# Chunk preparation of an RWKV-7 mixer in three batches, with heads alternating between the row halves of TensorE

## The chip, the cores and the metric

One core of a Trainium2 chip. The metric is the device time of one launch in microseconds (us), median of several runs.

## The reference, cut to what matters

Two layers; in each a token mixer of three groups of heads (stick-breaking attention, latent attention, RWKV-7) over 1024 tokens, and then a gated feed-forward block. The change concerns the RWKV-7 group, 8 heads of 64 channels:

```python
def step(state, inp):
    r_t, w_t, k_t, v_t, kk_t, a_t = inp
    sa = jnp.einsum('bhvk,bhk->bhv', state, -kk_t)
    state = (state * w_t[:, :, None, :] + sa[..., None] * (kk_t * a_t)[:, :, None, :]
             + v_t[..., None] * k_t[:, :, None, :])
    return state, jnp.einsum('bhvk,bhk->bhv', state, r_t)
_, ys = lax.scan(step, init, (tm(rh), tm(wh), tm(kh), tm(vh), tm(kk), tm(ah)))
```

## The kernel before, in words

The recurrence is computed in chunks of 64 tokens. `phase_a` does, for each of four head pairs (`ft`, two heads of 64 channels, one on partitions 0 to 63 and one on 64 to 127): projections of k, r and v (`proj_rw`, lines 202 to 204, matmuls of 512 columns into the tiles `psmm`), `rw_prep`, and then `rw_stage1` twice, once for each half of the sequence (`hf`, 8 chunks). After ft 1 and ft 3, `rw_inv` inverts the triangular blocks of four heads, mostly on VectorE (DVE), in pieces that stand between later projections. `rw_chain` runs the recurrence over chunks afterwards, and reads from DRAM what stage 1 and the inverse stored.

`rw_stage1` first forms decayed keys and queries on DVE, GpSimd (POOL) and ScalarE (ACT): AR (queries) and BK (keys), lines 612 to 638. Then comes the part that the change touches. A call handles two groups `g` of four chunks:

- lines 647, 648: transposes of the queries and a centred transpose of v, into one PSUM tile; ACT copies it to X (line 651) and Vt, a part of Vz (line 652);
- line 655: four transposes of the keys; ACT copies them to RB (line 657);
- line 662, the key-query products: for each head `h` four matmuls with 64 contraction rows, rows 0 to 63 for one head and 64 to 127 for the other, into a PSUM tile of that head; DVE multiplies them by the mask into Aa (line 665) and RB (line 666);
- line 674, 64x64 products of Aa and Vt, eight, which alternate between the two row halves (`e`), into one tile; ACT copies them to X (line 676);
- lines 680, 681: stores of RB and X, and after both groups line 685: stores of Vz, all issued by SyncE (SP).

An fp32 matmul that is no transpose is two passes, and the profile lists the passes: 512 for 256 matmuls. PSUM tiles of this part come from `ps2`, four buffers in all: the tags pa, py, pa, pq in turn.

```python
    def ps2(self):
        self.rot = (self.rot + 1) % 4
        return self.pst(("pa", "py", "pa", "pq")[self.rot])
```

The order on each engine is set when the kernel is built: a scheduler takes instructions of all running steps by priority and expected readiness. The projections of the next head pair fill PE between the steps of stage 1. Engines then run their own list in order.

Of the kernel before, what the change touches and what calls it, by code (L numbers as in the profile page):

```python
# [12 lines left out]
ALU = mybir.AluOpType  # L13
# [4 lines left out]
P = 128  # L18
# [12 lines left out]
C = 64  # L31
NCH = S // C
HC = NCH // 2
# [36 lines left out]
class Body:  # L70
# [31 lines left out]
    def ps1(self):  # L102
        return self.pst("ps")
# [419 lines left out]
    def mla_block(self, i, pr, hp, qk, V, wp):  # L523
# [9 lines left out]
        for u, (a0, a1) in enumerate(pcs):  # L533
# [6 lines left out]
            c = lambda o, u=u: st[:, o + u : o + u + 1]  # L540
            nc.vector.reduce_max(c(0), s, axis=AX.X)
            if u:
# [58 lines left out]
    def rw_stage1(self, ft, hf, rkv, prep, Aa, tp):  # L601
        nc = self.nc
        tk = slice(hf * W2, hf * W2 + W2)
        pr_, pk, pvv = (t[:, tk] for t in rkv)
        L_, av, kk = (t[:, tk] for t in prep)
        ps1 = self.ps2
        Vz = self.Vz[0]
        Vt = Vz.rearrange("p (j x) -> p j x", x=2 * P)[:, :, C : C + P]
        c3 = lambda t: t.rearrange("p (c i) -> p c i", i=C)
        pv4 = lambda t: t.rearrange("p (j e i) -> p j e i", e=2, i=C)  # L610
        G, iG = self.q2(tp), self.q2(tp)
        nc.vector.tensor_scalar(L_, L_, 1.0, None, op0=ALU.add)
        nc.vector.tensor_tensor_scan(L_, self.m01, L_, 0.0, op0=ALU.mult, op1=ALU.add)
        nc.scalar.activation(G, L_, AF.Exp, scale=-0.5 * EC)
        nc.scalar.activation(iG, L_, AF.Exp, scale=0.5 * EC)
        nc.gpsimd.tensor_copy(self.Gc[:, hf * HC : hf * HC + HC, ft], c3(G)[:, :, C - 1])
        AR = self.q4(tp).rearrange("p (a j e i) -> p a j e i", a=2, e=2, i=C)
        BK = self.q4(tp).rearrange("p (j e x i) -> p j e x i", e=2, x=2, i=C)
        kk4, G4, iG4 = pv4(kk), pv4(G), pv4(iG)
        for e in range(2):  # L620
            s_ = 1 - e
            nc.vector.scalar_tensor_tensor(AR[:, 0, :, s_, 1:C], kk4[:, :, e, 1:C], -1.0, G4[:, :, e, 0 : C - 1], op0=ALU.mult, op1=ALU.mult)
            nc.vector.tensor_scalar(AR[:, 0, :, s_, 0:1], kk4[:, :, e, 0:1], -1.0, None, op0=ALU.mult)
            nc.gpsimd.tensor_tensor(AR[:, 1, :, s_, :], pv4(pr_)[:, :, e, :], G4[:, :, e, :], op=ALU.mult)
        nc.sync.dma_start(self.ard[4 * hf : 4 * hf + 4, :, ft].rearrange("j p t -> p j t"), AR[:, 1].rearrange("p j e i -> p j (e i)"))
        nc.vector.scalar_tensor_tensor(kk, av, 1.0, kk, op0=ALU.add, op1=ALU.mult)
        for e in range(2):
            nc.vector.scalar_tensor_tensor(BK[:, :, 1 - e, 1 - e, :], kk4[:, :, e, :], 0.5, iG4[:, :, e, :], op0=ALU.mult, op1=ALU.mult)
        nc.scalar.activation(av, av, AF.Identity, scale=self.om[:, 18 + ft : 19 + ft], bias=self.om[:, 14 + ft : 15 + ft])
        nc.vector.tensor_tensor(av, av, pk, op=ALU.mult)  # L630
        for e in range(2):
            nc.vector.tensor_tensor(BK[:, :, 1 - e, e, :], pv4(av)[:, :, e, :], iG4[:, :, e, :], op=ALU.mult)
        nc.vector.scalar_tensor_tensor(av, pr_, self.pp("rwkv_r_k", ft), av, op0=ALU.mult, op1=ALU.mult)
        ps = ps1()
        self.bsum(ps, av, tp)
        bv = self.q2(tp)
        nc.vector.tensor_tensor(bv, ps, pvv, op=ALU.mult)
        nc.sync.dma_start(self.bvd[4 * hf : 4 * hf + 4, :, ft].rearrange("j p t -> p j t"), bv.rearrange("p (j t) -> p j t", t=P))
        flat = lambda t: t.rearrange("p a i -> p (a i)")
        for g in range(2):  # L640
            js = slice(2 * g, 2 * g + 2)
            RB = self.t(tp, [P, 2, 4, P], "RB", bufs=2)
            X = self.t(tp, [P, 2, 2, P], "X", bufs=2)
            pt = ps1()
            for q in range(2):
                j = 2 * g + q
                nc.tensor.transpose(pt[:, q * P : q * P + P], flat(AR[:, 0, j]), self.ident)
                nc.tensor.matmul(pt[:, (2 + q) * P : (3 + q) * P], pvv[:, j * P : j * P + P], self.cent, start=True, stop=True)
            pa = pt[:, 0:256].rearrange("p (q h k) -> p h q k", q=2, h=2)
            for h in range(2):  # L650
                nc.scalar.copy(X[:, h, :, h * C : h * C + C], pa[:, h])
            nc.scalar.copy(Vt[:, js, :], pt[:, 256:512].rearrange("p (q v) -> p q v", q=2))
            pb = ps1()
            for cc in range(4):
                nc.tensor.transpose(pb[:, cc * P : cc * P + P], flat(BK[:, 2 * g + cc // 2, cc % 2]), self.ident)
            pbv = pb.rearrange("p (c h k) -> p h c k", c=4, h=2)
            nc.scalar.copy(RB[:, :, :, C:P], pbv)
            for h in range(2):
                hr = slice(h * C, h * C + C)
                pA = ps1()  # L660
                for cc in range(4):
                    nc.tensor.matmul(pA[:, cc * P : cc * P + P], flat(BK[hr, 2 * g + cc // 2, cc % 2]), AR[hr, :, 2 * g + cc // 2, cc % 2, :], start=True, stop=True)
                pAv = pA.rearrange("p (c x) -> p c x", x=P)
                mk = self.maskA
                nc.vector.tensor_tensor(Aa[:, h, HC * hf + 4 * g : HC * hf + 4 * g + 4, :], pAv[:, :, 0:C], mk[:, None, 0:C].to_broadcast([P, 4, C]), op=ALU.mult)
                nc.vector.tensor_tensor(RB[:, h, :, 0:C], pAv[:, :, C:P], mk[:, None, C:P].to_broadcast([P, 4, C]), op=ALU.mult)
            pkv = ps1()[:, :256].rearrange("p (h q v) -> p h q v", h=2, q=2)
            for h in range(2):
                for q in range(2):
                    j = 2 * g + q  # L670
                    for e in range(2):
                        kr = slice(64 - 64 * e, 128 - 64 * e)
                        orow = slice(64 * e, 64 * e + 64)
                        nc.tensor.matmul(pkv[orow, h, q, :], Aa[kr, h, HC * hf + 2 * j + e, :], Vt[kr, j, h * C : h * C + C], start=True, stop=True)
            for h in range(2):
                nc.scalar.copy(X[:, h, :, C - h * C : P - h * C], pkv[:, h])
            gj = slice(4 * hf + 2 * g, 4 * hf + 2 * g + 2)
            RBv = RB.rearrange("p h (j e) x -> p h j (e x)", e=2)
            for h in range(2):
                nc.sync.dma_start(self.rbd[gj, :, 2 * ft + h].rearrange("j p x -> p j x"), RBv[:, h])  # L680
                nc.sync.dma_start(self.xxd[gj, :, 2 * ft + h].rearrange("j p x -> p j x"), X[:, h])
        for e in range(2):
            kr = slice(64 - 64 * e, 128 - 64 * e)
            for h in range(2):
                nc.sync.dma_start(self.psd[4 * hf : 4 * hf + 4, kr, 2 * ft + h, e, :].rearrange("j p x -> p j x"), Vz.rearrange("p (j h x) -> p j h x", h=2, x=P)[kr, :, h, :])

    def rw_inv(self, st, tp, Aa):
# [17 lines left out]
        mul = lambda o, x, y: nc.vector.tensor_tensor(o, x, y, op=ALU.mult)  # L705
        red = lambda o, x: nc.vector.tensor_reduce(o, x, axis=AX.X, op=ALU.add)
        for t in range(1, 16):
# [91 lines left out]
    def rw_chain_q(self, st, j, tp):  # L799
        nc = self.nc  # L800
        hs = slice(4 * st, 4 * st + 4)
        fs = slice(2 * st, 2 * st + 2)
        RB = self.t(self.tl, [P, 4, 2, P], "RBl", bufs=2)
        PS = self.t(self.tl, [P, 4, 2, P], "PSl", bufs=2)
        arl = self.t(self.tl, [P, 2, 2, C], "arl", bufs=2)
        bvl = self.t(self.tl, [P, 2, P], "bvl", bufs=Y_LAG + 2)
        nc.sync.dma_start(PS.rearrange("p h e x -> p h (e x)"), self.psd[j, :, hs].rearrange("p h e x -> p h (e x)"))
        nc.sync.dma_start(RB.rearrange("p h e x -> p h (e x)"), self.rbd[j, :, hs])
        nc.sync.dma_start(arl, self.ard[j, :, fs].rearrange("p f (e i) -> p f e i", e=2))
        nc.sync.dma_start(bvl, self.bvd[j, :, fs])  # L810
        QC = self.t(tp, [P, 2, 2, 2, P], "QC", bufs=2)
        PSh = PS.rearrange("p (f h) e x -> p f h e x", h=2)
        RBh = RB.rearrange("p (f h) c x -> p f h c x", h=2)
        for h in range(2):
# [35 lines left out]
    def rw_chain_y1(self, pY, tp):  # L850
# [6 lines left out]
        nc.scalar.activation(yq, ys, AF.Square)  # L857
        nc.vector.tensor_reduce(vs, yq, axis=AX.X, op=ALU.add)
        nc.vector.tensor_scalar(vs, vs, 1.0 / C, GN_EPS, op0=ALU.mult, op1=ALU.add)
# [369 lines left out]
```

## Time and profile before

| | |
|---|---|
| median of 3 runs | 3166.87 us (3161.5 to 3167.62) |
| span of the profiled execution, first to last instruction | 3156.8 us |
| time of that execution beside its span | not given by itself; the median of the runs lies 10.1 us above the span |
| PE busy | 3030.5 us, 96% |
| DVE busy | 1796.4 us, 57% |
| ACT busy | 1060.2 us, 34% |
| mean granted clock of TensorE | 0.984 |

An engine's busy time is the union of its instructions. The profile gives the start of each pass on PE; ends are modelled, so the distance from start to start tells what a pass costs in a row. In rows of the timeline, neighbours of one line and tile are merged (x8), and in brackets stands the idle time of the engine before the first of them, with what ended it.

### The profile page before, as it was taken

To read this page: it belongs to the slowest core of one execution; us is meant where nothing else is said; L and a number is where in the kernel's file an instruction comes from. 1 tells how busy PE (TensorE), PEld (TensorE's weight loads), DVE (VectorE), ACT (ScalarE), POOL (GpSimd) and SP (SyncE) were. 2 spreads that over 40 slices of the span, in tenths; PEclk is the share of its full clock that TensorE was granted. 3 is DMA by queue.
4 is the path that set the end of the run, shared out by engine and by line. 5 is a ranking of instruction groups with operands and counts; after the bars stand their busy time and mean duration, and the time that the engine had idled before them with its cause. 6 is when DMAs were issued, how large, how long until landed. Compare 5 with 4: busy or idle time off the path is not lost. (4 is left out here: it accounts for less than half of the span.)

```text
span 3156.8 us, 42014 instructions
## 1 busy us (share of the span) xinstructions
PE 3030.5 (96%) x16572; PEld 2405.0 (76%) x16572; DVE 1796.4 (57%) x2842; ACT 1060.2 (34%) x1865; POOL 329.9 (10%) x346
## 2 busy tenths in 40 slices
PE   8998999998999999999999989999999999999998
PEld 6676777766888888888877767777668888888887
DVE  4577764777644444444746877567765444344436
ACT  5444343754122111222244443456532211121210
POOL 0112131022000000000001211311310000000000
PEclk9999999999999999999999999999999999999999
DMA  4344666323421111111124356661244111111111
GB/s 129 106 132 117 186 181 185 84 60 122 144 92 47 54 40 47 54 48 53 62 86 124 104 139 192 178 195 46 68 133 172 55 47 40 41 56 51 54 47 54
DMA packets 339284, 301.79 MB, mean 96 GB/s; under 512 B 25224, under 2 KB 304016, under 8 KB 339088
## 3 DMA queue, kind: packets, MB, share of 16 engines
q1 hardware_dynamic: 339088, 299.11, 31.9%
q8 instruction: 131, 2.15, 0.3%
q14 instruction: 65, 0.53, 0.1%
HBM read 208.87 MB, written 90.18 MB: 95 GB/s over the span
## 5 line engine op out<-in xcount | busy, mean ns | idle before, releaser
L202 PE MATMUL psmm<-xTh,whi 128*128 128x512 f32 x2144 | 851.8, 397 | 0.0
L203 PE MATMUL psmm<-xTl,whi 128*128 128x512 f32 x2144 | 851.6, 397 | 0.0
L204 PE MATMUL psmm<-xTh,wlo 128*128 128x512 f32 x2144 | 851.3, 397 | 0.0
L197 ACT CAST whi<-raw 128x1024 fp32r<-128x1024 f32 x152 | 159.9, 1052 | 1108.4 <-PE psmm L203 1085.6
L204 PEld LDWEIGHTS psmm<-xTh,wlo 128*128 128x128 f32 x2144 | 404.9, 189 | 92.8 <-issue 4.4
L203 PEld LDWEIGHTS psmm<-xTl,whi 128*128 128x128 f32 x2144 | 404.9, 189 | 92.7 <-issue 3.9
L202 PEld LDWEIGHTS psmm<-xTh,whi 128*128 128x128 f32 x2144 | 404.5, 189 | 92.8 <-issue 4.4
L198 DVE TENSOR_TENSOR wlo<-raw,whi 128x1024 fp32r<-128x1024 f32 x122 | 148.9, 1220 | 422.1 <-ACT whi L197 422.0
L1031 DVE TENSOR_TENSOR y<-y,psps 128x512 f32<-128x512 f32 x288 | 196.5, 687 | 171.7 <-PE psps L204 171.3
L202 PE MATMUL psps<-wdh,hh 128*128 128x512 f32 x672 | 266.8, 397 | 0.0
L203 PE MATMUL psps<-wdl,hh 128*128 128x512 f32 x672 | 263.1, 391 | 0.0
L204 PE MATMUL psps<-wdh,hl 128*128 128x512 f32 x672 | 260.1, 391 | 0.0
L894 POOL TENSOR_TENSOR lrs<-lrs,mhalf 128x1 f32<-128x1 f32 x32 | 29.1, 910 | 1639.8 <-DVE lrs L893 1639.8
L202 PEld LDWEIGHTS psps<-wdh,hh 128*128 128x128 f32 x672 | 126.1, 188 | 36.6 <-ACT hh L197 5.5
L204 PEld LDWEIGHTS psps<-wdh,hl 128*128 128x128 f32 x672 | 126.1, 188 | 27.1
L203 PEld LDWEIGHTS psps<-wdl,hh 128*128 128x128 f32 x672 | 126.3, 188 | 25.8
L1006 DVE TENSOR_TENSOR cv<-cv,psmm 128x1024 f32<-128x1024 f32 x44 | 53.8, 1222 | 141.9 <-PE psmm L204 136.9
L198 DVE TENSOR_TENSOR wdl<-raw,wdh 128x1024 fp32r<-128x1024 f32 x42 | 51.5, 1225 | 89.9 <-ACT wdh L197 89.9
L198 POOL TENSOR_TENSOR wlo<-raw,whi 128x1024 fp32r<-128x1024 f32 x30 | 75.8, 2528 | 243.5 <-ACT whi L197 243.5
L820 PE MATMUL pspa<-RBl,PSl 128*128 128x128 f32 x512 | 74.6, 295 | 16.5 <-ACT QC L823 10.8
L312 PE MATMUL pspa<-Aa,mv 128*64 128x128 f32 x576 | 84.6, 288 | 4.7 <-ACT Aa L328 4.5
L203 PE MATMUL psmm<-wol,whi 128*128 128x512 f32 x192 | 77.3, 403 | 8.8 <-DVE wol L198 4.6
(443 smaller groups left out, 4757.1 us busy)
## 6 DMA issues: line engine op xcount, KB each, us to landing
raw<-in_ffn_w_up_dram SPq DMA_DIRECT2D x88, 512.0 KB
raw<-in_w_in_dram SPq DMA_DIRECT2D x44, 512.0 KB
raw<-in_ffn_w_down_dram SPq DMA_DIRECT2D x44, 512.0 KB
rbd<-RB SPq DMA_DIRECT2D x64, 256.0 KB
PSl<-psd SPq DMA_DIRECT2D x32, 512.0 KB
RBl<-rbd SPq DMA_DIRECT2D x32, 512.0 KB
psd<-Vz SPq DMA_DIRECT2D x64, 128.0 KB
xxd<-X SPq DMA_DIRECT2D x64, 128.0 KB
```

The costliest lines, as they stand in the source:

```text
L197: self.nc.scalar.copy(hi, src)
L198: (eng or self.nc.vector).tensor_tensor(lo, src, hi.bitcast(F32), op=ALU.subtract)
L202: mm(out, lh, rh, start=start, stop=False)
L203: mm(out, lh, rl, start=False, stop=False)
L204: mm(out, ll, rh, start=False, stop=stop)
L312: self.nc.tensor.matmul(av[hp * 64 : hp * 64 + 64, :], V[:, j, hcol : hcol + 64], wt[:, j, :], start=j == 0, stop=j == nb - 1)
L820: nc.tensor.matmul(pQ[:, f, e, :], PSh[:, f, h, e, :], RBh[:, f, h, e, :], start=True, stop=True)
L894: nc.gpsimd.tensor_tensor(rs, rs, self.mhalf[:, 0:1], op=ALU.pow)
L1006: nc.vector.tensor_tensor(cv, cv, pg, op=ALU.mult)
L1031: nc.vector.tensor_tensor(y[:, i, hs], y[:, i, hs], ps, op=ALU.add)
```

## The change

Both groups are now handled in three batches. RB and X of both groups are taken first. Batch 1: the transposes of both groups. Batch 2: all four key-query tiles of a call are taken at once, and the loop over chunks is outside that over heads, so that heads alternate. Batch 3: the 64x64 products of both groups go into two tiles, one for each `e`; ACT copies each tile's 64 rows by group and head, eight copies a call where there were four of 128 rows. The stores come last.

```diff
+        RBs = [self.t(tp, [P, 2, 4, P], "RB", bufs=2) for _ in range(2)]
+        Xs = [self.t(tp, [P, 2, 2, P], "X", bufs=2) for _ in range(2)]
         for g in range(2):
             js = slice(2 * g, 2 * g + 2)
-            RB = self.t(tp, [P, 2, 4, P], "RB", bufs=2)
-            X = self.t(tp, [P, 2, 2, P], "X", bufs=2)
+            RB, X = RBs[g], Xs[g]
...
+        mk = self.maskA
+        pAs = [[ps1() for h in range(2)] for g in range(2)]
+        for g in range(2):
+            for cc in range(4):
+                for h in range(2):
+                    hr = slice(h * C, h * C + C)
+                    nc.tensor.matmul(pAs[g][h][:, cc * P : cc * P + P], flat(BK[hr, 2 * g + cc // 2, cc % 2]), AR[hr, :, 2 * g + cc // 2, cc % 2, :], start=True, stop=True)
             for h in range(2):
-                hr = slice(h * C, h * C + C)
-                pA = ps1()
-                for cc in range(4):
-                    nc.tensor.matmul(pA[:, cc * P : cc * P + P], flat(BK[hr, 2 * g + cc // 2, cc % 2]), AR[hr, :, 2 * g + cc // 2, cc % 2, :], start=True, stop=True)
...
-            pkv = ps1()[:, :256].rearrange("p (h q v) -> p h q v", h=2, q=2)
+        pks = [ps1() for e in range(2)]
+        for g in range(2):
             for h in range(2):
                 for q in range(2):
-                    j = 2 * g + q
                     for e in range(2):
+                        j = 2 * g + q
                         kr = slice(64 - 64 * e, 128 - 64 * e)
-                        orow = slice(64 * e, 64 * e + 64)
-                        nc.tensor.matmul(pkv[orow, h, q, :], Aa[kr, h, HC * hf + 2 * j + e, :], Vt[kr, j, h * C : h * C + C], start=True, stop=True)
-            for h in range(2):
-                nc.scalar.copy(X[:, h, :, C - h * C : P - h * C], pkv[:, h])
+                        o = ((g * 2 + h) * 2 + q) * C
+                        nc.tensor.matmul(pks[e][64 * e : 64 * e + 64, o : o + C], Aa[kr, h, HC * hf + 2 * j + e, :], Vt[kr, j, h * C : h * C + C], start=True, stop=True)
+        for e in range(2):
+            er = slice(64 * e, 64 * e + 64)
+            pkv = pks[e].rearrange("p (g h q v) -> p g h q v", g=2, h=2, q=2)
+            for g in range(2):
+                for h in range(2):
+                    nc.scalar.copy(Xs[g][er, h, :, C - h * C : P - h * C], pkv[er, g, h])
+        for g in range(2):
```

In the changed file the lines are 648, 649 and 656 (transposes), 652, 653 and 657 (their copies), 664 (key-query), 667 and 668 (masks), 677 (64x64) and 683 (their copies).

What the scheduler makes of it is seen in the order of instructions on each engine. A number behind a tile's name tells buffers apart; in brackets stand the engines whose semaphores an instruction waits for, where it waits. First PE in the first half of ft 1, layer 0, from the last transposes of the keys on (pspa_1654 is head 0's key-query tile, pspy_1661 head 1's). Before:

```order
L655 MATMUL pspq_1648<-ident_60,q_299_1612 128x128 x4
L662 MATMUL pspa_1654<-q_298_1611,q_299_1612 128x128 [waits Pool_49]
L662 MATMUL pspa_1654<-q_298_1611,q_299_1612 128x128 x3
L662 MATMUL pspy_1661<-q_298_1611,q_299_1612 128x128 [waits DVE_49]
L662 MATMUL pspy_1661<-q_298_1611,q_299_1612 128x128 x3
L674 MATMUL pspa_1668<-Vz_182_875,Aa_877 64x64 [waits DVE_49,Activation_49]
L674 MATMUL pspa_1668<-Vz_182_875,Aa_877 64x64 x3
L647 MATMUL pspq_1685<-ident_60,q_298_1611 128x128 [waits Activation_49]
L648 MATMUL pspq_1685<-cent_79,pst_1546 128x128
L674 MATMUL pspa_1668<-Vz_182_875,Aa_877 64x64 [waits DVE_49]
L674 MATMUL pspa_1668<-Vz_182_875,Aa_877 64x64 x3
```

The change:

```order
L656 MATMUL pspy_1672<-ident_60,q_299_1620 128x128 [waits DVE_49]
L656 MATMUL pspy_1672<-ident_60,q_299_1620 128x128 x3
L664 MATMUL pspa_1678<-q_298_1619,q_299_1620 128x128 [waits PE_49,Activation_49,Pool_49]
L664 MATMUL pspq_1679<-q_298_1619,q_299_1620 128x128 [waits Activation_49]
L664 MATMUL pspa_1678<-q_298_1619,q_299_1620 128x128
L664 MATMUL pspq_1679<-q_298_1619,q_299_1620 128x128
L664 MATMUL pspa_1678<-q_298_1619,q_299_1620 128x128
L664 MATMUL pspq_1679<-q_298_1619,q_299_1620 128x128
L664 MATMUL pspa_1678<-q_298_1619,q_299_1620 128x128
L664 MATMUL pspq_1679<-q_298_1619,q_299_1620 128x128
L664 MATMUL pspa_1680<-q_298_1619,q_299_1620 128x128 [waits PE_49,Activation_49]
L664 MATMUL pspy_1681<-q_298_1619,q_299_1620 128x128 [waits Activation_49]
```

Four of one head and four of the other have become pairs, 16 in a row, and no transpose stands between the 64x64 products any more. ft 3 is set out in the same way.

Second, PE in the first half of ft 0, layer 0, from the key-query matmuls on. Before:

```order
L662 MATMUL pspa_1163<-q_220_1120,q_221_1121 128x128 [waits Pool_49]
L662 MATMUL pspa_1163<-q_220_1120,q_221_1121 128x128 x3
L647 MATMUL pspq_1194<-ident_60,q_220_1120 128x128 [waits Activation_49]
L648 MATMUL pspq_1194<-cent_79,pst_1055 128x128
L575 MATMUL pspy_1137<-q_223_1138,bonesr_78 128x512 [waits Activation_49]
L647 MATMUL pspq_1194<-ident_60,q_220_1120 128x128
L674 MATMUL pspa_1177<-Vz_182_875,Aa_877 64x64 [waits DVE_49]
L674 MATMUL pspa_1177<-Vz_182_875,Aa_877 64x64 x3
```

The change:

```order
L664 MATMUL pspa_1179<-q_220_1120,q_221_1121 128x128 [waits PE_49,Activation_49,Pool_49]
L664 MATMUL pspa_1179<-q_220_1120,q_221_1121 128x128 x3
L664 MATMUL pspq_1180<-q_220_1120,q_221_1121 128x128 [waits Activation_49]
L664 MATMUL pspq_1180<-q_220_1120,q_221_1121 128x128
L575 MATMUL pspy_1137<-q_223_1138,bonesr_78 128x512 [waits Activation_49]
L664 MATMUL pspq_1180<-q_220_1120,q_221_1121 128x128 x2
L664 MATMUL pspa_1181<-q_220_1120,q_221_1121 128x128
L576 MATMUL pspy_1137<-q_224_1139,bonesr_78 128x512 [waits DVE_49]
L664 MATMUL pspa_1181<-q_220_1120,q_221_1121 128x128 x3
L677 MATMUL pspa_1207<-Vz_182_875,Aa_877 64x64 [waits DVE_49,PE_49]
```

Here the scheduler still puts a whole head ahead of the other, with sums of another step (lines 575, 576) between; the source alternates, the list does not.

Third, ACT in the first half of ft 0, layer 0, of the change, from the second copy of v to the end of that half (Vz holds v, RB_1147 and RB_1148 are the two groups' tiles):

```order
L653 COPY Vz_182_875<-pspa_1165 128x2x128
L197 CAST whi_1549<-raw_1548 128x1024
L657 COPY RB_1147<-pspq_1159 128x8x64
L197 CAST q_223_1138<-ta_943 128x512
L302 ACTIVATE pst_1383<-psmm_1413,om_69_293 128x512
L614 ACTIVATE q_240_1245<-tw_942 128x512
L615 ACTIVATE q_241_1246<-tw_942 128x512
L657 COPY RB_1148<-pspy_1173 128x8x64
L683 COPY X_1149<-pspa_1207 64x2x64 x2
L683 COPY X_1150<-pspa_1207 64x2x64 x2
L683 COPY X_1149<-pspq_1208 64x2x64 x2
L683 COPY X_1150<-pspq_1208 64x2x64 x2
```

A weight cast (line 197) stands ahead of the copy to RB that frees a PSUM buffer for the key-query matmuls, and the eight copies of 64 rows stand together at the end.

## Rows read from the trace of the kernel before

**Rows 1.** The page, busy time by engine.

```profile
PE 3030.5 (96%) x16572; PEld 2405.0 (76%) x16572; DVE 1796.4 (57%) x2842; ACT 1060.2 (34%) x1865; POOL 329.9 (10%) x346
```

**Rows 2.** Table by stretch (us: length, busy by engine, granted clock, DMA share, GB/s).

```profile
143.00:173.00 30.00, 28.40 (x220) 22.26 (x221) 23.50 (x46) 16.98 (x40) 4.51 (x4) 1.00 0.60 173
189.00:215.00 26.00, 24.66 (x206) 19.80 (x205) 18.03 (x35) 11.22 (x31) 4.17 (x4) 1.00 0.67 197
215.00:253.00 38.00, 31.89 (x131) 24.79 (x130) 36.36 (x60) 15.21 (x19) 6.83 (x5) 0.91 0.18 46
336.00:362.00 26.00, 24.60 (x205) 19.77 (x204) 18.57 (x34) 10.96 (x31) 7.65 (x18) 1.00 0.68 202
```

**Rows 3.** Timeline of PE, first half of ft 1 (start us, length us, instruction).

```profile
191.02 0.82 PE L662 MATMUL pspa<-q,q 64*128 64x128 f32 x5
191.57 0.37 PE L662 MATMUL pspy<-q,q 64*128 64x128 f32 x1
191.68 0.27 PE L662 MATMUL pspa<-q,q 64*128 64x128 f32 x1
191.79 0.27 PE L662 MATMUL pspy<-q,q 64*128 64x128 f32 x1
...
192.01 0.72 PE L662 MATMUL pspy<-q,q 64*128 64x128 f32 x5
193.96 0.45 PE L674 MATMUL pspa<-Vz,Aa 64*64 64x64 f32 x8 [1.23 <-DVE Aa L665]
194.34 0.33 PE L647 MATMUL pspq<-ident,q 128*128 128x128 f32 x1
```

**Rows 4.** Timeline of PE, second half of ft 1, one head between projections.

```profile
202.86 0.40 PE L204 MATMUL psmm<-xTh,wlo 128*128 128x512 f32 x1
203.09 0.40 PE L202 MATMUL psmm<-xTh,whi 128*128 128x512 f32 x1
203.42 1.16 PE L662 MATMUL pspq<-q,q 64*128 64x128 f32 x8
204.51 0.50 PE L203 MATMUL psmm<-xTl,whi 128*128 128x512 f32 x1
204.84 0.40 PE L204 MATMUL psmm<-xTh,wlo 128*128 128x512 f32 x1
205.08 0.39 PE L575 MATMUL pspa<-q,bonesr 128*128 128x512 f32 x1
```

**Rows 5.** Timeline of PE, first half of ft 0, 64x64 products.

```profile
156.18 0.68 PE L674 MATMUL pspq<-Vz,Aa 64*64 64x64 f32 x16
156.79 0.50 PE L202 MATMUL psmm<-xTh,whi 128*128 128x512 f32 x1
```

**Rows 6.** Timeline of DVE, masks of the first half of ft 1.

```profile
193.40 0.41 DVE L665 TENSOR_TENSOR Aa<-pspa,maskA 128x256 f32<-128x256 f32 x1
193.73 0.41 DVE L666 TENSOR_TENSOR RB<-pspa,maskA 128x256 f32<-128x256 f32 x1
...
197.31 0.42 DVE L665 TENSOR_TENSOR Aa<-pspy,maskA 128x256 f32<-128x256 f32 x1 [2.51 <-PE pspy L662]
...
198.31 0.42 DVE L666 TENSOR_TENSOR RB<-pspa,maskA 128x256 f32<-128x256 f32 x1
```

**Rows 7.** Timeline of ACT, copies of ft 1.

```profile
190.85 0.42 ACT L651 COPY X<-pspa 128x128 f32<-128x128 f32 x2
...
191.42 0.62 ACT L657 COPY RB<-pspq 128x512 f32<-128x512 f32 x1
...
195.31 0.43 ACT L676 COPY X<-pspa 128x128 f32<-128x128 f32 x2 [2.23 <-PE pspa L674]
...
205.94 0.59 ACT L657 COPY RB<-pspa 128x512 f32<-128x512 f32 x1 [0.94 <-PE pspa L655]
```

**Rows 8.** Groups of PE: line, tiles, shape, count, busy us, mean ns, idle before.

```profile
L674 PE MATMUL pspa<-Vz,Aa 64*64 64x64 f32 x256 | 14.3, 229 | 8.3 <-DVE Aa L665 7.9
```

**Rows 9.** Timeline of SP, a store of RB in the first half of ft 1.

```profile
200.16 0.44 SPq L680 DMA_DIRECT2D rbd<-RB  x1
```

More of the change, by code (lines that the diff above doesn't have):

```diff
@@ L655, in rw_stage1 @@
                 nc.tensor.transpose(pb[:, cc * P : cc * P + P], flat(BK[:, 2 * g + cc // 2, cc % 2]), self.ident)
-            pbv = pb.rearrange("p (c h k) -> p h c k", c=4, h=2)
-            nc.scalar.copy(RB[:, :, :, C:P], pbv)
-            for h in range(2):
-                hr = slice(h * C, h * C + C)
-                pA = ps1()
-                for cc in range(4):
-                    nc.tensor.matmul(pA[:, cc * P : cc * P + P], flat(BK[hr, 2 * g + cc // 2, cc % 2]), AR[hr, :, 2 * g + cc // 2, cc % 2, :], start=True, stop=True)
-                pAv = pA.rearrange("p (c x) -> p c x", x=P)
-                mk = self.maskA
+            nc.scalar.copy(RB[:, :, :, C:P], pb.rearrange("p (c h k) -> p h c k", c=4, h=2))
@@ new lines, in rw_stage1 @@
+        mk = self.maskA
[5 more added lines that the diff above has]
+                    nc.tensor.matmul(pAs[g][h][:, cc * P : cc * P + P], flat(BK[hr, 2 * g + cc // 2, cc % 2]), AR[hr, :, 2 * g + cc // 2, cc % 2, :], start=True, stop=True)
+            for h in range(2):
+                pAv = pAs[g][h].rearrange("p (c x) -> p c x", x=P)
@@ L665, in rw_stage1 @@
                 nc.vector.tensor_tensor(Aa[:, h, HC * hf + 4 * g : HC * hf + 4 * g + 4, :], pAv[:, :, 0:C], mk[:, None, 0:C].to_broadcast([P, 4, C]), op=ALU.mult)
-                nc.vector.tensor_tensor(RB[:, h, :, 0:C], pAv[:, :, C:P], mk[:, None, C:P].to_broadcast([P, 4, C]), op=ALU.mult)
-            pkv = ps1()[:, :256].rearrange("p (h q v) -> p h q v", h=2, q=2)
+                nc.vector.tensor_tensor(RBs[g][:, h, :, 0:C], pAv[:, :, C:P], mk[:, None, C:P].to_broadcast([P, 4, C]), op=ALU.mult)
@@ L677, in rw_stage1 @@
+        for g in range(2):
             gj = slice(4 * hf + 2 * g, 4 * hf + 2 * g + 2)
-            RBv = RB.rearrange("p h (j e) x -> p h j (e x)", e=2)
+            RBv = RBs[g].rearrange("p h (j e) x -> p h j (e x)", e=2)
             for h in range(2):
                 nc.sync.dma_start(self.rbd[gj, :, 2 * ft + h].rearrange("j p x -> p j x"), RBv[:, h])
-                nc.sync.dma_start(self.xxd[gj, :, 2 * ft + h].rearrange("j p x -> p j x"), X[:, h])
+                nc.sync.dma_start(self.xxd[gj, :, 2 * ft + h].rearrange("j p x -> p j x"), Xs[g][:, h])
```

## The prediction

> **What bounds the kernel now.** I read the page's busy shares first: TensorE (PE) is busy for 96% of the span [rows 1], so what shortens PE's queue, or a wait in front of it, shortens the kernel, and nothing else does by itself. The changed function runs 16 times (two layers, four head pairs ft, two halves hf of the sequence), in pairs of calls that I call bursts. The table by stretch shows three bursts and the stretch behind the second [rows 2]: inside a burst PE is busy for 24.7 of 26 us, so a burst is PE's own work; in 215 to 253 us DVE is busy for 36.4 of 38 us and PE for 31.9, at a granted clock of 0.91 of 2.4 GHz, which means short spells at 1.2 GHz. There DVE's block inverse leads, and it can start only when the burst's last mask is done. A burst that ends sooner on both engines is therefore worth its full length; one that ends sooner on PE alone is not.
>
> PE's instructions one by one come next, for the first half of ft 1. A key-query matmul is two passes, 64 rows of the array each; the passes of one head start 0.11 us apart, and the second head's first pass (191.57, tile pspy) starts while four passes of the first head are still to be run [rows 3]. The two row halves run side by side, and a half that is free starts up to four passes early. So four matmuls of one head behind four of the other take 1.55 us (191.02 to 192.46, and the last 0.11), not 1.9. One head alone takes 1.09 us from its first pass to the next instruction, of which 0.89 is eight passes. The rest is change of shape: matmuls of 512 columns stand 0.23 apart, but 0.33 ahead of the 64-row ones and again behind the first of the next shape [rows 4]. Each change of array shape costs two times 0.10 us, 0.10 ahead of it and 0.10 behind its first pass.
>
> The 64x64 products are paired already: 16 passes end 0.61 us after the first starts, 8 passes 0.38 (193.96 to 194.34) [rows 5, 3], so eight more cost 0.23, which is 0.058 a pair.
>
> **The change part by part.** I count on PE's listing of both kernels, since the listing and not the source says who stands beside whom.
>
> 1. *Key-query matmuls.* Of 256, 20 stand directly behind one of the other head before, 116 now, but unevenly. With 0.112 us a pass and 0.10 for the first of each half: the first half of ft 1 or ft 3 goes from two stretches of 4+4, 2 x 1.54 = 3.08 us, to one fully alternating stretch of 16 matmuls, 16 passes deep, 1.89. The second half goes from 0.99 + 0.99 + 1.54 = 3.53 to 0.77 (a stretch of three) + 1.89 (thirteen, eight of them on one head) = 2.66. Each such burst saves 2.06, four of them 8.2. In ft 0 and ft 2 the scheduler still sets out whole heads: 7.18 to 6.83 and 7.16 to 7.27 a burst, together 0.5 less over both layers. Sum: -8.7.
> 2. *Changes of shape* at the lines of the key-query and 64x64 products: 190 before, 156 now, 34 x 0.20 = 6.8; of that 0.8 lies in item 1 (48 stretches became 40). Sum: -6.0.
> 3. *64x64 products*: in 16 places the two row halves no longer stand next to each other in the listing, 16 x 0.116 = +1.9. The new second PSUM tile itself gives nothing, as they are paired already. Both halves write one tile before the change, and still start as pairs. The Trainium skill (TensorEngine Tiling (Array Packing), Gotcha 1: PSUM Pressure) says that different row tiles cannot access one PSUM bank at the same time; by that rule the split would bring these products a pairing that they lack. The trace does not agree: 64 columns at 0.112 / 128 us each are 0.056, so two passes in 0.058 are side by side.
> 4. *Masks on DVE*: the same 128 instructions. In the first half of ft 1 the first mask starts at 193.40, held by DVE's own work before it, and the last at 198.31, after 2.51 us of waiting for the second group's matmuls [rows 6]. With both groups' matmuls ahead, eight masks 0.33 apart start last at 195.7: 2.6 us sooner. So DVE follows PE in ft 1 and ft 3 and gives the saving on to the block inverse.
> 5. *Copies on ACT*: 64 more, of 64 rows x 128 elements, which the trace does not show. From below they cost nothing where ACT is idle; from above 0.27 each as the 128-row ones alone, 17 us in all; those 128-row ones come 0.16 apart in a row. I take nothing on the path: ACT sat idle for 2.23 us before such a copy [rows 7]. With that cover gone, the tiles of the 64x64 products come free some 0.3 to 0.6 us later in each call, at most 16 x 0.6 = 10 us.
> 6. *Waits in front of key-query matmuls.* All four PSUM buffers now go to the second batch, so it waits for ACT's copies of both groups. One group's copies take 1.2 us (190.85 to 192.04) [rows 7], two 2.4, done at 193.2; the first eight alternating matmuls, begun when one group is copied, end at 193.0. I take 0.1 to 0.5 us a call, against the waits of 1.2 us that PE has now in front of the 64x64 products, 7.9 us in six places [rows 3, 8], which go where masks come earlier. I set the two equal: 0, with -8 and +16 (1 us a call) as ends.
> 7. *Transfers*: the same number and size. The last store of RB of the first half is issued at 200.16, and ACT fills the next RB of the second half from 205.9 on [rows 9, 7]; masks that end 2.6 us sooner lengthen that distance. I cost it at nothing.
>
> Sum: -8.7 - 6.0 + 1.9 = -12.8 us. The profiled execution would go from a span of 3156.8 to 3144.0; the median of the runs stands 10.1 above that span, so I predict 3154.0 us. The first item leans on rows: by the Trainium skill (TensorE: Matmul & The Clock Gate, Part 3) matmuls start strictly in program order, which the pass at 191.57 contradicts; by that rule the kernel before would have fewer passes side by side, and item 1 would be -9.8 (44 matmuls of 0.223 us).
>
> **The rivals.**
> - *The saved PE time comes back as waits.* Masks (eight at 0.33, 2.7 us a call) take longer than alternating matmuls (1.9), so PE reaches the 64x64 products early and waits. For it: that wait exists today in front of them [rows 8]. Against it: items of filler stand between them, and DVE itself waited 2.5 us for PE [rows 6]. Then items 1 and 3 fall away, and of item 2 some two thirds stay: about 3163. The Trainium skill says that row tiling speeds up TensorE and not the emptying of PSUM (TensorEngine Tiling (Array Packing), PSUM Bottleneck); that is this rival. Chance 0.22.
> - *Slower: four buffers are too few.* The second batch cannot begin until ACT has emptied the first, and in the listing ACT puts a weight cast ahead of one of those copies in ft 0, and PE's queue stands behind it. It decides from 0.8 us a call on (12.8 / 16). At 1.5 us a call it is +24 - 12.8 = +11: 3178. For it: PE is in order, and ACT now has 64 more copies there. Against it: ACT is busy for 11 of 26 us in ft 1 [rows 2]. Chance 0.12.
> - *More than the sum.* PE's present waits go without new ones (-5 to -8), and shorter idle keeps the clock at 2.4 GHz behind the bursts, where 9% of 38 us were lost in this stretch alone [rows 2]: 3141. Should the 64x64 products nevertheless gain from a tile for each half, by half of their 512 passes at 0.029 us, it is another 7 us: 0.02 of this case. Chance 0.14.
>
> **How the numbers follow.** The forecast, 3154 give or take 6, gets 0.52. About 0.2% (6 us, also the spread of the three runs) is what a measurement of this kernel can tell from no change: faster takes the forecast and the larger gain, 0.66; same is the first rival, 0.22; slower the second, 0.12. The range goes from 3138, the larger gain with some room, to 3168, which takes in the first rival and leaves out most of the second.
>
> **What would show it.** Right: in ft 1 and ft 3 key-query passes of two tiles start in pairs, 16 matmuls in about 1.9 us; the last mask of a burst comes 2 to 4 us sooner after its first transpose; PE's busy time falls by about 10 us or more; bursts of ft 0 and ft 2 stay as they are. Wrong: waits of PE for ACT in front of the key-query line of over 0.8 us a call, or waits in front of the 64x64 products that grow by what the matmuls saved.

## The result, and the profile after

| | before | after |
|---|---|---|
| median on one chip, us | 3161.5 (7 runs, 3154.0 to 3167.7) | 3178.75 (7 runs, 3170.2 to 3183.4) |
| ratio, 95% interval | | 1.0051 [1.0038, 1.0065] |
| span of the profiled execution, us | 3156.8 | 3177.0 |
| mean granted clock of TensorE | 0.984 | 0.976 |

The change makes the kernel 0.5% slower. The forecast was 3154 us, and 3178.75 lies outside the range of 3138 to 3168.

Busy time by engine on the page after, which answers to [rows 1]:

```profile
PE 3050.0 (96%) x16572; PEld 2420.3 (76%) x16572; DVE 1788.1 (56%) x2842; ACT 1069.4 (34%) x1929; POOL 329.3 (10%) x346
```

PE has the same 16572 instructions and is busy for 19.5 us longer, almost the whole 20.2 us of the span. So over the whole kernel the passes have become longer; PE's idle time hardly changes (127.0 us, where it was 126.3).

The first half of ft 1 went nearly as forecast. PE's timeline after, first half of ft 1, answers to [rows 3]:

```profile
199.42 0.60 PE L656 MATMUL pspy<-ident,q 128*128 128x128 f32 x4
199.95 0.37 PE L664 MATMUL pspa<-q,q 64*128 64x128 f32 x1
199.96 0.37 PE L664 MATMUL pspq<-q,q 64*128 64x128 f32 x1
200.16 0.27 PE L664 MATMUL pspa<-q,q 64*128 64x128 f32 x1
200.17 0.27 PE L664 MATMUL pspq<-q,q 64*128 64x128 f32 x1
...
201.78 0.38 PE L664 MATMUL pspy<-q,q 64*128 64x128 f32 x2
202.11 0.30 PE L677 MATMUL pspa<-Vz,Aa 64*64 64x64 f32 x2
```

Passes of the two heads start 0.01 us apart, and all 16 key-query matmuls take 2.16 us up to the next instruction (forecast: about 1.9). DVE's masks answer to [rows 6]; they now stand in a row, without the 2.51 us wait:

```profile
201.23 0.41 DVE L667 TENSOR_TENSOR Aa<-pspa,maskA 128x256 f32<-128x256 f32 x1
...
203.21 0.41 DVE L667 TENSOR_TENSOR Aa<-pspy,maskA 128x256 f32<-128x256 f32 x1
203.54 0.41 DVE L668 TENSOR_TENSOR RB<-pspy,maskA 128x256 f32<-128x256 f32 x1
```

From this half's first transpose to the start of its last mask it is 5.9 us (197.66 to 203.54), where it was 8.5 (189.83 to 198.31).

The first half of ft 0 did not. The table by stretch (us: length, busy by engine, granted clock, DMA share, GB/s) over the first 22 us of ft 0, before and then after:

```profile
143.00:151.00 8.00, 6.45 (x44) 5.17 (x45) 7.81 (x12) 4.15 (x8) 2.70 (x1) 1.00 0.10 18
151.00:165.00 14.00, 14.00 (x104) 10.98 (x103) 10.76 (x25) 8.27 (x20) 1.80 (x3) 1.00 0.76 220
```

```profile
143.00:151.00 8.00, 6.34 (x43) 5.10 (x43) 6.73 (x15) 5.71 (x13) 2.97 (x2) 1.00 0.30 66
151.00:165.00 14.00, 14.00 (x65) 10.43 (x65) 6.79 (x18) 3.34 (x11) 1.59 (x2) 0.51 0.48 148
```

PE is busy for all 14 us in both, but it gets through 65 instructions where it was 104, at a granted clock of 0.51, that is 1.2 GHz of 2.4 for nearly the whole stretch (151.3 to 165.0 us). PE's timeline after shows what stood ahead of the fall at 151.3 us:

```profile
146.90 0.66 PE L656 MATMUL pspq<-ident,q 128*128 128x128 f32 x4
147.49 0.93 PE L664 MATMUL pspa<-q,q 64*128 64x128 f32 x6
...
148.87 0.50 PE L575 MATMUL pspy<-q,bonesr 128*128 128x512 f32 x1
...
150.77 0.50 PE L576 MATMUL pspy<-q,bonesr 128*128 128x512 f32 x1 [0.76 <-DVE q L198]
151.21 1.13 PE L664 MATMUL pspa<-q,q 64*128 64x128 f32 x4
...
152.70 1.11 PE L677 MATMUL pspa<-Vz,Aa 64*64 64x64 f32 x8
...
157.89 2.07 PE L664 MATMUL pspy<-q,q 64*128 64x128 f32 x8
```

From 146.90 to 151.2 stand four transposes, 18 passes of 64 rows, two matmuls of 512 columns and one wait of 0.76 us. The queries' transposes of both groups are done by then; before the change those of the second group, 64x64 products and projections stood among these passes. Behind the fall eight key-query passes take 2.0 us (157.89 to the next instruction at 159.90), where one head took 1.09 [rows 4], and DVE waits for them, 5.72 us in all, with the other work that stands ahead of them:

```profile
160.00 0.42 DVE L667 TENSOR_TENSOR Aa<-pspy,maskA 128x256 f32<-128x256 f32 x1 [5.72 <-PE pspy L664]
```

Where the 20.2 us came from, by the starts of the first transposes, the chain's first matmul (L820 before, L828 after) and the first matmul of the latent attention, in the two profiled executions; in brackets the time at 1.2 GHz within the stretch:

| stretch | layer 0 before | after | layer 1 before | after |
|---|---|---|---|---|
| ft 0 to ft 1 | 46.7 (0) | 53.8 (13.7) | 47.9 (3.4) | 53.7 (13.7) |
| ft 1 to ft 2 | 63.2 (6.8) | 60.8 (6.8) | 63.4 (10.2) | 59.3 (6.8) |
| ft 2 to ft 3 | 83.1 (10.2) | 84.5 (13.7) | 83.7 (10.2) | 88.6 (23.9) |
| ft 3 to the chain | 36.8 (0) | 33.9 (0) | 37.0 (0) | 34.5 (0) |
| the chain stretch | 173.1 (10.2) | 179.0 (17.1) | 165.9 (6.8) | 172.6 (17.1) |

The stretches that begin with ft 1 and ft 3 gain 11.9 us. Those of ft 0 and ft 2 lose 19.2, and the chain stretch, whose code is the same, loses 12.6. That is 19.9 of the 20.2. Each column is one execution, and where the clock falls differs between executions; the runs below repeat these stretches in other kernels.

### The profile page after: what moved, and what is told of

Same layout as the page of the kernel before. It is cut to its first block, busy times and chain, and to the rows that moved or that the text cites. A ratio compares the mean times of both kernels' runs of the same rounds, so it can differ in the third digit from the quotient of the medians.

```text
span 3177.0 us, 42078 instructions
## 1 busy us (share of the span) xinstructions
PE 3050.0 (96%) x16572; PEld 2420.3 (76%) x16572; DVE 1788.1 (56%) x2842; ACT 1069.4 (34%) x1929; POOL 329.3 (10%) x346
## 5 line engine op out<-in xcount | busy, mean ns | idle before, releaser
L203 PEld LDWEIGHTS psps<-wdl,hh 128*128 128x128 f32 x672 | 126.3, 188 | 25.7
L1014 DVE TENSOR_TENSOR cv<-cv,psmm 128x1024 f32<-128x1024 f32 x44 | 53.7, 1221 | 143.9 <-PE psmm L204 138.9
L828 PE MATMUL pspa<-RBl,PSl 128*128 128x128 f32 x512 | 73.5, 293 | 18.8 <-ACT QC L831 12.8
L312 PE MATMUL pspa<-Aa,mv 128*64 128x128 f32 x576 | 84.5, 288 | 4.7 <-ACT Aa L328 4.5
L828 PEld LDWEIGHTS pspa<-RBl,PSl 128*128 128x128 f32 x512 | 66.4, 201 | 27.2 <-ACT QC L831 15.5
```

The source lines that it names most:

```text
L203: mm(out, lh, rl, start=False, stop=False)
L312: self.nc.tensor.matmul(av[hp * 64 : hp * 64 + 64, :], V[:, j, hcol : hcol + 64], wt[:, j, :], start=j == 0, stop=j == nb - 1)
L828: nc.tensor.matmul(pQ[:, f, e, :], PSh[:, f, h, e, :], RBh[:, f, h, e, :], start=True, stop=True)
L1014: nc.vector.tensor_tensor(cv, cv, pg, op=ALU.mult)
```

## The experiments

Theory A: the change gains in ft 1 and ft 3, and loses in ft 0 and ft 2 because the clock falls there. Rivals: B, four PSUM buffers are too few (the prediction's second rival), so that each call waits; C, what is worse is the order that the scheduler gives to later steps, the chain above all. The ratios below are to the kernel before on the same chip; chips differ by a few us, so runs are compared by their ratios.

**The change in ft 1 and ft 3 only**, and then **in ft 0 and ft 2 only** (`ft % 2 == 0` in the condition). Lines without a mark are the old code, moved to the right.

```diff
+        if ft % 2:
+            RBs = [self.t(tp, [P, 2, 4, P], "RB", bufs=2) for _ in range(2)]
...
+        else:
             for g in range(2):
                 js = slice(2 * g, 2 * g + 2)
                 RB = self.t(tp, [P, 2, 4, P], "RB", bufs=2)
...
```

> The new code for ft 1 and 3 only, the old code for ft 0 and 2. Theory A (the change gains about 3 us in each burst of ft 1 and ft 3 and loses in ft 0 and ft 2, where the clock falls to 1.2 GHz): faster than before, 4 bursts x 2.8 = 11 us less, about 3150 where before has 3161, ratio 0.996 to 0.998; no long half-clock stretch near 151 and 1725 us. Theory B (four buffers are too few, each call waits): slower than before, some half of the 17 us, about 3170. Theory C (the order of later steps, above all of the chain, is what is worse): no faster than before, with the chain stretch of the second inverse still some 4 us longer in each layer.

> The new code for ft 0 and 2 only, the old code for ft 1 and 3. Theory A: slower than the whole change, 17 + 11 = about 28 us above before, 3185 to 3190, with half-clock stretches near 151 and 1725 us. Theory B: about 3170, half of the loss. Theory C: depends on the chain; the burst of ft 0 itself is no longer than before by more than 2 us.

Measured: 3154.6 us, ratio 0.9982 [0.997, 0.9993], and 3178.7, 1.0057 [1.0036, 1.0078]. The loss goes with the new code in ft 0 and ft 2, as A has it, though the second run lost 18 us and not the 28 that A expected. B falls: it lets every call lose. But the first run gained 6 us, about half of the 11 expected. In its profile the stretches from ft 0 to the chain are 7.3 and 7.9 us shorter than before, and the chain stretch is 4.8 and 4.5 longer, which is C's mark. In the run with ft 0 and ft 2 the chain stretch is about that of before (175.2 and 165.8).

**Alternation alone**, group by group as before:

```diff
-            for h in range(2):
-                hr = slice(h * C, h * C + C)
-                pA = ps1()
-                for cc in range(4):
+            pAs = [ps1() for h in range(2)]
+            for cc in range(4):
+                for h in range(2):
+                    hr = slice(h * C, h * C + C)
...
```

> Alternation alone: in each group the two key-query tiles are taken together and heads alternate; groups follow each other as before, one tile for the 64x64 products. Theory A: the gain of the pairs (4 x about 0.45 us a burst in ft 1 and ft 3, a little in ft 0 and ft 2) without the loss of ft 0, so 3150 to 3158 where before has 3161. Theory B: no loss either, since a group's second batch needs two buffers of four; 3155 to 3161. Theory C: anything between 3150 and 3180, with the chain as the place.

**Batches alone**, the changed kernel with the loops swapped:

```diff
-            for cc in range(4):
-                for h in range(2):
+            for h in range(2):
+                for cc in range(4):
```

> Three batches as in the change, but head 0's four matmuls of a group before head 1's. Theory A: the loss of ft 0 and ft 2 stays, the gain of ft 1 and ft 3 falls by some 1 to 2 us a burst: 3180 to 3188. Theory B: the same, since the buffers are the same. If alternation itself did the harm (its 64-row matmuls leave the array half as long busy), it would be faster than the change: 3160 to 3170.

Measured: 3155.9, 0.9979 [0.9965, 0.9992], and 3155.4, 0.9988 [0.9975, 1.0002]. The second was missed by both theories: two loops swapped take 0.6%, some 20 us, off the changed kernel. The expectation's last case, that alternation itself does the harm, had the direction, but not the size (3160 to 3170). The steps ahead of the chain give little of it. From ft 0 to the chain it takes 232.0 and 232.1 us, the changed kernel 233.0 and 236.2, and its clock falls in ft 0 as well. Its chain stretch is 169.0 and 162.2, against 179.0 and 172.6. So the order of later steps can carry the sign, and the next runs asked what sets it.

**The change in ft 1 only, and in ft 3 only** (the conditions `ft == 1` and `ft == 3`).

> The new code for ft 1 only. In the run with ft 1 and ft 3 the bursts and what lies between them gave 6 to 8 us a layer, and the chain stretch behind ft 3 took 5 back. Theory C1 (the new order in ft 3's burst is what changes the order of the second inverse against the chain): here the chain stretch is as before (173 and 166 us from the chain's first matmul to the latent attention's), the bursts give 3 to 4 us a layer, together 6 to 8 us faster, ratio about 0.998. Theory C2 (any change upstream does it): the chain stretch is again 5 us longer, no gain.

> The new code for ft 3 only. Theory C1: the burst gives 3 us a layer, the chain stretch takes 5: 3160 to 3165, no faster than before, with a half-clock stretch in the chain near 445 and 2015 us. Theory C2 or none: 3 us a layer faster, 3154.

Measured: 3153.6, 0.9988 [0.9977, 0.9999], and 3157.9, 1.001 [0.9999, 1.0021]. With ft 1 alone the chain stretch stays (173.9 and 166.1); with ft 3 alone it grows (176.3 and 169.5) and eats what the burst gained. C1 holds for the chain; the first run's gain, 4 us, is again about half of the 6 to 8 expected (its profiled execution, 3160.6 us, was its slowest, with 10.2 us at 1.2 GHz between ft 3 and the chain of layer 0 and 13.7 in ft 0 of layer 1). The listings say the same: from the first to the last query product of the chain, the sequence of lines and operations on PE and on DVE takes one of four forms in all kernels of this study, and only the code of ft 3 decides which.

| order of the chain, by ft 3's code | runs | chain stretch, layer 0 | layer 1 | of it at 1.2 GHz |
|---|---|---|---|---|
| the code before | before and two | 173.1 to 175.2 | 165.8 to 166.1 | 10.2; 6.8 |
| alternation alone | one | 171.9 | 166.7 | 6.8; 6.8 |
| the change | after and four | 176.3 to 179.0 | 168.7 to 172.6 | 13.7 to 17.1; 10.2 to 17.1 |
| batches, whole heads | four (three of them below) | 169.0 to 172.4 | 162.2 to 164.7 | 3.4 to 10.2; 3.4 to 6.8 |

The change's range lies above that of the code before in both layers, that of whole heads below it. In layer 0 the gaps are small (1.1 and 0.7 us), and alternation alone is one run. This allows a forecast for kernels that had not run:

**The whole change, but whole heads in ft 3.**

```diff
+        if ft == 3:
...
+                for h in range(2):
+                    hr = slice(h * C, h * C + C)
+                    for cc in range(4):
...
+        else:
...
                 for cc in range(4):
                     for h in range(2):
                         hr = slice(h * C, h * C + C)
...
```

> The whole change with one loop swapped back in ft 3 alone: three batches there too, but head 0's four matmuls of a group before head 1's. By the listings the order on TensorE and VectorE from the first to the last matmul of the chain's query products is one of four, and only the code of ft 3 decides which: as before, as in the change, as with alternation alone, as with whole heads in batches. Theory C1 (this order is what the chain stretch costs): the stretch from the chain's first matmul to the latent attention's goes from 179.0 and 172.6 us in the whole change to about 169 and 162, as in the run with whole heads; in all 18 to 20 us faster than the whole change, about 3158 to 3161, no slower than before. Rival (the chain's loss comes from what the burst in ft 0 and ft 2 did to clock and transfers upstream): 3175 to 3180.

Measured: 3155.1, 0.9993 [0.9978, 1.0008]. Two loops swapped in one of four head pairs, and the kernel is no longer slower than before, 0.6% (18 us) under the changed kernel's ratio of 1.0051. The 18 to 20 us were expected with a chain stretch of about 169 and 162; it came to 172.4 and 164.7, which is 14.5 us less than in the changed kernel, so some of the 18 lies elsewhere. In the profiles another 7.3 us stand ahead of the chain of layer 1, most of them where ft 2, whose code is that of the changed kernel, had 10.2 us at 1.2 GHz instead of 23.9. The table by stretch shows the chain stretch of layer 0 in the changed kernel, and then in this one:

```profile
376.90:555.90 179.00, 163.57 (x1423) 131.48 (x1424) 102.70 (x226) 64.08 (x123) 40.71 (x37) 0.95 0.59 179
```

```profile
375.80:548.20 172.40, 158.35 (x1425) 126.27 (x1425) 100.66 (x221) 64.22 (x124) 42.01 (x37) 0.99 0.59 185
```

Both start within 1.1 us of each other. PE is busy 5.2 us longer in the first, at 0.95 instead of 0.99, and idle 1.4 us longer. In the changed kernel the clock falls three times within this stretch, at 383.4, 451.7 and 550.7 us, for 6.8, 6.8 and 3.4 us; the kernel before has falls near its start and end too (380.2 and 540.6), and the one in the middle is new. PE's timeline there; L760 is the inverse, L855 the chain:

```profile
446.48 0.40 PE L202 MATMUL psmm<-xTh,whi 128*128 128x512 f32 x1
448.24 0.76 PE L760 MATMUL pspi<-Aa,pd 32*32 32x32 f32 x36 [1.36 <-DVE Aa L751]
448.93 0.33 PE L855 MATMUL pspy<-S,QC 128*64 128x64 f32 x2
449.19 0.24 PE L760 MATMUL pspi<-Aa,pd 32*32 32x32 f32 x2
...
451.79 0.31 PE L760 MATMUL pspi<-Aa,pd 32*32 32x32 f32 x2
452.03 0.47 PE L855 MATMUL pspy<-S,QC 128*64 128x64 f32 x2
```

and the same place with whole heads in ft 3 (L812 the inverse, L880 and L899 the chain):

```profile
443.03 1.13 PE L880 MATMUL pspa<-RBl,PSl 128*128 128x128 f32 x8 [0.29 <-DVE mo L941]
443.92 0.47 PE L203 MATMUL psmm<-xTl,whi 128*128 128x512 f32 x1
444.93 1.07 PE L812 MATMUL pspi<-Aa,pd 32*32 32x32 f32 x54 [0.54 <-DVE Aa L803]
446.25 0.45 PE L899 MATMUL pspy<-S,QC 128*64 128x64 f32 x8 [0.26 <-DVE S L902]
```

In the first, 1.4 us of waiting and then 4.7 us of small matmuls, 36 of the inverse and then turns of two with the chain. In the second, the waits are shorter, 54 of them stand in a row, and query products of 128x128 are right ahead. Why the scheduler comes to the one or the other from a different last burst was not followed up.

**Is the clock a cause or only goes along?** In ft 0 and ft 2 one matmul of 512 columns was put into each key-query tile ahead of its own, which overwrite it:

```diff
+            if ft % 2 == 0:
+                for h in range(2):
+                    nc.tensor.matmul(pAs[g][h], self.identr, self.lora[0][:, 0:512], start=True, stop=True)
```

> The whole change, and in ft 0 and ft 2 one matmul of 512 columns into each key-query tile ahead of its key-query matmuls, which overwrite it: 32 more matmuls of 0.23 us, 7.4 us of pure extra work. Theory A (the clock is what the change loses in ft 0 and ft 2): these bring PE's array to work there; the half-clock stretches at 151 us (13.7 us), 1725 us (13.7) and 1868 us (13.7) shrink or go, worth up to 20 us together, so the kernel is no slower than the whole change and probably 5 to 12 us faster, 3167 to 3175. Theory B (waits for buffers, or the order alone): 7 to 10 us slower than the whole change, 3186 to 3189, the low stretches being a consequence of the waits. In both the chain stretch stays some 5 us a layer longer than before.

Measured: 3178.8, 1.0072 [1.006, 1.0084]; by ratio that is 0.2%, some 7 us, above the changed kernel, with intervals that just overlap. In total time A, which expected 5 to 12 us less, was wrong, and B's 7 to 10 us more came nearer; the profile has to tell why. The first 22 us of ft 0:

```profile
143.00:151.00 8.00, 7.67 (x49) 5.97 (x50) 5.90 (x14) 5.12 (x12) 0.20 (x1) 1.00 0.26 56
151.00:165.00 14.00, 12.19 (x91) 9.28 (x92) 11.43 (x22) 6.61 (x19) 4.15 (x3) 1.00 0.67 194
```

The fall is gone from ft 0, in both layers, and from first transpose to first transpose the first half takes 15.2 us, where the changed kernel took 20.1 and 19.4 and the kernel before 14.6 and 16.1. So in this half of ft 0 the clock is the loss, and the fall goes when PE is given these matmuls. As a repair it is worthless. The stretch from ft 0 to ft 1 takes 51.3 us at full clock, with PE busy for 49.5 against 45.2 before: of these 4.3 us the eight added matmuls are 1.8 at 0.23 each, and the rest was not taken apart. In ft 2 the time at 1.2 GHz came to 17.1 us in both layers (13.7 and 23.9 in the changed kernel), so what makes the loss there was not shown by this run.

What the fall costs is seen without any edit. Up to ft 1 the runs with the change in ft 1 only and in ft 1 and ft 3 have the same order on PE, the kernel's before. In layer 1 the clock fell in the first of them, and not in the other:

```profile
1707.40:1759.70 52.30, 50.79 (x292) 40.61 (x293) 36.87 (x67) 26.99 (x52) 8.70 (x8) 0.87 0.45 121
```

```profile
1706.90:1753.20 46.30, 44.75 (x292) 35.66 (x293) 36.85 (x67) 27.03 (x52) 8.71 (x8) 1.00 0.52 137
```

13.7 us at 1.2 GHz cost 6.0 us, 0.44 us for each. By the Trainium skill (TensorE: Matmul & The Clock Gate, Part 1) time at half clock costs half of itself; that gives an estimate of 6.9, and the trace agrees roughly. So with the old order the clock can fall too, but seldom does: of twelve stretches of ft 0 with the old code two had over 4 us at 1.2 GHz. With the change, whole heads in batches, or one tile for the products it was nine of ten. With alternation alone it was none of two, so the fall goes with the batches and not with the alternation.

**One tile for the 64x64 products** of a group, and four copies on ACT as before, the rest as changed.

```diff
-        pks = [ps1() for e in range(2)]
+        for g in range(2):
+            pkv = ps1()[:, :256].rearrange("p (h q v) -> p h q v", h=2, q=2)
```

> The whole change, but the 64x64 products of a group in one tile with four copies a call on ACT, as before the change. Theory A: the 64 extra copies and the split matter little; within 5 us of the whole change, 3174 to 3182. If the two tiles and the eight copies were what costs (each tile waits for both groups' masks), it is faster by 8 us or more: below 3171.

Measured: 3170.0, 1.0042 [1.0026, 1.0059], an interval that overlaps the changed kernel's [1.0038, 1.0065]. Its 3170 us lie just under the 3171 that was to speak for a cost of the copies, but by ratio it is 0.09%, some 3 us, under the changed kernel, where 8 were asked. So the 64 copies and the second tile are at most a side issue; up to some 0.1% for them stays open. In layer 1 the clock did not fall in ft 0, and that stretch took 46.8 us, as before the change: in this order the batches cost nothing where the clock stays up.

**Two kernels put together from this**: old code in ft 0 and ft 2, whole heads in batches in ft 3, and in ft 1 either the change or whole heads too. The second is the run with batches alone, with one condition more:

```diff
+        if ft % 2:
             RBs = [self.t(tp, [P, 2, 4, P], "RB", bufs=2) for _ in range(2)]
...
                 for h in range(2):
                     hr = slice(h * C, h * C + C)
                     for cc in range(4):
...
+        else:
+            for g in range(2):
...
```

> Old code in ft 0 and ft 2, the change in ft 1, three batches with whole heads in ft 3. Theory A and C1 together: the bursts and what lies between give 6 to 8 us a layer as in the run with ft 1 and ft 3, the chain stretch gives 4 a layer as with whole heads: 20 to 24 us faster than before, 3134 to 3142, ratio 0.9925 to 0.9945. Rival (gains do not add, the chain's order is worth something only behind the other bursts): 3150 to 3157.

> Old code in ft 0 and ft 2, three batches with whole heads in ft 1 and ft 3. Batching gave 2.9 us in a burst of ft 1 with whole heads too, though its 16 key-query matmuls take 2.8 us where alternating ones take 2.2. Theory: within 4 us of the run with the change in ft 1 and whole heads in ft 3: 3134 to 3145. If alternation is what gains in ft 1: some 3 us a layer slower than that run.

Measured: 3141.3, 0.9949 [0.9936, 0.9963], and 3139.5, 0.9942 [0.9927, 0.9956]. Gains of bursts and of the chain's order add up, if not fully: the first run is 16 us faster than before, where 20 to 24 were expected, and its ratio is just above the 0.9925 to 0.9945 forecast. The second run, within 4 us of the first as expected, beats both kernels, by 0.6% and 1.1%, and it has no alternating heads at all. Its busy times:

```profile
PE 3017.1 (96%) x16572; PEld 2396.5 (76%) x16572; DVE 1792.4 (57%) x2842; ACT 1063.3 (34%) x1897; POOL 332.4 (11%) x346
```

PE's 13.4 us less against [rows 1] are close to the 12.8 that the change was forecast to save, but by another way: part of them is the chain, which the forecast left out.

## Why the prediction was wrong

- *Item 1, key-query matmuls: right in size, in the wrong part.* In the first half of ft 1 they went from 1.71 + 1.71 to 2.21 us (first start to last modelled end), 1.21 less; forecast was 1.19. By the forecast's own measure, with the last pass at 0.11 us, it is 3.10 to 2.05, 1.05 less. With whole heads in batches it is 2.82: half of the saving comes from the batch, half from alternation. Alternation's half is worth nothing in time here: from the first half's first transpose to the second's it is 8.0 us with it, 7.6 without, 10.5 before. In that one point the first rival, saved PE time that comes back, was right.
- *Item 4, masks: right.* The last mask of this half comes 2.6 us sooner after its first transpose, as forecast, and the stretches from ft 1 and ft 3 gain 2.4 to 4.1 us each, 11.9 in all. In the largest, 4.1, 3.4 us less at 1.2 GHz have a part. Item 2, changes of shape, was not measured by itself.
- *Items 3 and 5, 64x64 products and copies: not contradicted.* The +1.9 of item 3 was not measured by itself. Two tiles give no pairing that one lacks: eight passes start within 0.23 us in either (204.25 to 204.48 after; 0.45 less the last pass's own 0.22 in [rows 3]), and the run with one tile and four copies was at most some 3 us faster.
- *Item 6, waits: set to 0, and too cautious.* The new waits that it allowed in front of the key-query matmuls did not come: the list of PE's waits after has no row for L664. Waits in front of the 64x64 products went from 7.9 us in six places [rows 8] to 2.4 (all rows of L677), which is the gain that the third rival named:

```profile
PE pspa L677 <- DVE RB L668: 1.0, 4, 0.2
PE pspy L677 <- DVE RB L668: 0.7, 2, 0.4
PE pspq L677 <- DVE RB L668: 0.7, 2, 0.4
```

- *"Bursts of ft 0 and ft 2 stay as they are": the step that failed first.* The listing showed that little changed there in how key-query passes stand side by side, and the sum priced each pass at 2.4 GHz. The clock was thought of only as something that shorter idle would keep up (third rival). What the runs showed is that the clock falls there: from ft 0 to the chain the two layers hold about 37.5 us more at 1.2 GHz than before. At 0.44 to 0.46 for each (the two runs above; eight passes that take 2.01 us instead of 1.09) that is some 17 us, against a change of +7.3 in all. By this estimate these stretches would be 9 to 10 us shorter without it, near the forecast sum; no run shows the changed order of ft 2 without such falls.
- *The sum ended at the last store of ft 3.* No item and no rival priced the steps that the scheduler places anew behind it, though their listing was there to be read. They cost 12.6 us: 17 us more at 1.2 GHz are 7.5 to 7.9 of it by the same estimate, and 4.9 are idle time of PE (3.2 and 1.7). Either loss decides the sign: with old code in ft 0 and ft 2 (0.9982), or with whole heads in ft 3 (0.9993), the kernel is no longer slower.
- *The second rival* named 3178 us, and its number came true by luck, without its mechanism: PE's waits show no wait for ACT in front of the key-query matmuls.
- *The test of PE's busy time*, "falls by about 10 us or more", was no test of the edit, since a pass at 1.2 GHz is busy for longer.
- *The step from span to median*, 10.1 us, leaned on three runs: over seven the median before stands 4.7 us above that span. So the forecast of 3154 stood some 5 us too high, and against the -12.8 of the sum the medians moved by +17.25.

## What to carry to other kernels

Where a scheduler orders the work, compare the listing to the end of the program, and not only at the changed lines: which later stretches come out identical and which do not tells where unpriced time can arise, and with a handful of runs each order can be given a price. Before packing small matmuls closer together, take from the rows at which clock each stretch runs, and read the new rows again for it: here ft 0 in batches mostly fell to 1.2 GHz and gave back more than the packing saved, while the burst of ft 1, packed more tightly, did not fall. When two edits come in one change, run each alone: here batches alone and alternation alone were each as fast as before or faster, and only the two together were slower.

## What had not been expected of the hardware

- The granted clock fell to 1.2 GHz while PE was busy. Between the first transposes at 143.9 us and the fall at 151.3 its longest wait was 0.76 us; the kernel before waited 1.44 us at this place and did not fall, as its timeline of PE below has it. (Both waited 1.67 us right ahead of the first transposes.) From 146.9 us to the fall stood narrow matmuls and two of 512 columns; with four more of 512 columns in each call of ft 0 and ft 2 it did not fall in ft 0. But narrow matmuls alone do not make it fall: in the first half of ft 1 of the same kernel stand only transposes, 64-row passes and 64x64 products for 5.9 us, with one wait of 0.36, and the clock stays at 2.4 GHz (the second row below). What sets the fall stays open. The Trainium skill (TensorE: Matmul & The Clock Gate, Part 1) lets the clock fall when the engine has stood idle, and tells of one kernel in which many short idles did it; the fall at 151.3 us agrees with neither closely, with one wait of 0.76 us.

```profile
150.12 0.45 PE L674 MATMUL pspa<-Vz,Aa 64*64 64x64 f32 x8 [1.44 <-DVE Aa L665]
```

```profile
197.66:203.58 5.92, 5.56 (x77) 5.10 (x75) 5.47 (x11) 4.34 (x12) 3.85 (x4) 1.00 0.42 112
```

- One and the same order on PE ran at either clock in ft 0 (46.3 and 52.3 us), so the order alone does not fix the clock; in these traces it changed how often ft 0 fell (two of twelve, nine of ten).
